# A residual stream kept token-major through both output projections, with the residual added by DMA

## The chip, the core and the metric

The kernel runs on one core of one Trainium2 chip. A core has a matrix engine (TensorE: PE in the profile, with PEld for the loading of its stationary operand), a vector engine (VectorE, DVE), a scalar engine (ScalarE, ACT), a general engine (GpSimd, POOL) and a sync engine (SyncE, SP) that here only issues DMAs. The metric is the device time of one execution in microseconds. Three runs of the kernel before took 2227.62, 2227.78 and 2229.94 us; their median is 2227.78 us.

## The reference

A trunk of two layers over 256 tokens of width D = 2048, in float32. `rms(x, w)` is x divided by the root of the mean of its squares, times the gains w.

```
h = x
h = h + (rms(gla(rms(h) @ w_in)) * silu(g)) @ gla_w_out     # gated linear attention, 4 heads
h = h + (silu(a) * u) @ w_down0     # a, u: the halves of a causal conv of width 3 over rms(h) @ w_up0
k, v = rms(h) @ kv_w                # shared keys and values, 16 heads of 128
q = rms(h) @ moba_w_q
h = h + softmax(q k' + bias) v @ moba_w_out                 # 256 tokens: own block only, causal
h = h + (silu(a) * u) @ w_down1
```

`gla_w_out` and `moba_w_out` are 2048 x 2048, each `w_up` is 2048 x 11264, each `w_down` 5632 x 2048.

## The kernel before

**Products.** Every weight is float32 and is used in two float32r parts: `whi`, the rounded weight, and `wlo`, what the rounding left. Activations are kept in the same two parts. A product takes three terms: hi x hi, lo x hi, hi x lo.

**The weight stream.** `WeightStream` (line 55) fetches weights from HBM in chunks of 128 x 2048 floats (1 MB) on SP's queue into three raw buffers. A chunk is split in halves of 1024 columns: ACT casts (line 126), DVE subtracts (line 127). Half n is what step n of the kernel multiplies; `step()` hands it out, and it runs the jobs that `after(n, job)` has put off by n steps. Halves are split two to three steps ahead. Chunk c + 4 is asked for when chunk c has been split.

**Two forms of product.** `gemm` (line 298) is feature-major: the weight is the stationary operand and the activations are streamed, hi and lo together as 512 columns against `whi` (line 305), then hi alone as 256 columns against `wlo` (line 307). A step is 8 + 8 matmuls, and four steps give 256 output features of all 256 tokens. `gemm_tok` (line 311) and `down` (line 625) are token-major: the activation is stationary and 512 weight columns are streamed, 12 matmuls a step.

`down` computes each down projection in two blocks of 1024 outputs. It takes the hidden features 256 at a time (index k, 22 of them). A plain k is 24 matmuls. A k marked with + in `ORDERS` uses a Strassen-like form of seven block products instead of eight: 21 matmuls, in four steps of 3, 6, 6 and 6. That form needs sums of the weight's quarters (`t13`, `t24`: `_sums`, lines 99 to 101, on DVE) and sums of the activation's quarters (`combine`, line 577, on DVE and ACT). The sums of accumulators that the form leaves are made after the last + (`u_sums`). The last k of a block, the tail, come in two passes (f = 0, 1), so that half of the outputs are complete before the other half.

**The residual.** It lives feature-major in `h` (eight pairs of 128 features, 256 tokens each). Both output projections, `go` and `mo`, use `gemm` in `project` (line 568), 8 x 4 steps each: `residual` adds the product into `h` with two DVE additions per pair, `make_xw` makes the next stage's operand from `h`, and `add_squares` sums squares over the pairs. The first down projection comes out token-major; `back` (line 762) turns it with 32 TensorE transposes, adds it into `h`, and `h` goes to DRAM (`hspill`) and comes back, since on-chip space is short meanwhile. In the second layer `turn_h` (line 715) turns `h` with 32 more transposes into DRAM (`hscr`), and `last_down` fetches it and adds it on DVE.

**The norms.** A `Norm` collects squares and makes the root as a row over tokens (`token_rstd`: a sum over partitions by a matmul with ones, then `rsqrt` with tables on ACT), as two columns (`column_rstd`), or both.

**Order of the work.** The order on an engine is not the program's alone: the file is planned by the language's scheduler, which issues what it holds ready first, earlier work preferred. SP carries the weight stream, POOL's queue the DMAs of `hspill`, `hscr` and the bias. PSUM gives three accumulators of two banks and two single banks. Large tiles come from one pool of 34 slots, small ones from a pool of six.

Of the kernel before, what the change touches and what calls it, by code (L numbers as in the profile page):

```python
# [37 lines left out]
def _order(text):  # L38

    return [(int(k.rstrip("+")), k.endswith("+")) for k in text.split()]  # L40
# [3 lines left out]
ORDERS = [[_order("0 2 4 1+ 6 3+ 8 5+ 10 7+ 12 16 9+ 14 11+ 17 13+ 18 15+ 19 20 21"),  # L44
           _order("0 2 4 6 8 1+ 10 3+ 12 5+ 14 7+ 16 9+ 17 11+ 18 13+ 19 15+ 20 21")],
          [_order("0 2 4 1+ 6 3+ 8 5+ 10 7+ 12 16 9+ 14 11+ 17 13+ 18 15+ 19 20 21"),
           _order("0 1+ 2 3+ 4 5+ 6 7+ 8 16 9+ 10 11+ 12 17 13+ 14 15+ 18 19 20 21")]]


def _tail(order):  # L50

    return min(3, len(order) - 1 - max(i for i, (_, seven) in enumerate(order) if seven))


class WeightStream:
# [19 lines left out]
    def add_quads(self, w, g, order):  # L75

        for i, (_, seven) in enumerate(order):
# [65 lines left out]
def trunk(ctx: ExitStack, tc: tile.TileContext, xT, cst, msk, w1p, w2a, w_k, w_qa, w_v2, w_v, w_g, w_go,  # L143
# [20 lines left out]
    def bank(name, shape):  # L164
        return mis_ps.tile(list(shape), F32, name=name, tag="bank")

    ws = WeightStream(tc, raw, parts)
    plan = [(w_v2, 1, 16384), (w_v, 2, 8192), (w_k, 4, 4096), (w_qa, 4, 4096), (w_g, 8, 4096), (w_go, 8, 4096),
            (w_up0, FT, 4096), (w_dn0, 2, None),
            (w_mq, 4, 8192), (w_kk, 4, 8192), (w_kv, 4, 8192), (w_mo, 8, 4096),  # L170
            (w_up1, FT, 4096), (w_dn1, 2, None)]
    for w, groups, cols in plan:
        for g in range(groups):
            if cols:
                ws.add(w, g, cols)
            else:
                ws.add_quads(w, g, ORDERS[int(w is w_dn1)][g])
# [7 lines left out]
    one = keep.tile([128, 1], F32, name="one")  # L185
# [3 lines left out]
    V.memset(one, 1.0)  # L189
# [4 lines left out]
    V.memset(mhalf, -0.5)  # L194
# [12 lines left out]
    def load_rest():  # L207
# [3 lines left out]
        nc.sync.dma_start(mk, msk)  # L211

    ws.lead[7, 0] = [load_rest]
# [7 lines left out]
    def make_xw(p, c, name):  # L221
        x = slot([128, 2, 2 * S], F32R, name)
        for i in range(2):
            n = col(c + 2 * p + i)
            hi = A.activation(x[:, i, :S], h[p][:, i, :], AF.Copy, scale=n)  # L225
            ws.first = ws.first or hi.ins
            V.scalar_tensor_tensor(x[:, i, S:], h[p][:, i, :], n, x[:, i, :S].bitcast(F32),
                                   op0=OP.mult, op1=OP.subtract)
        return x

    def add_squares(p, acc):
        if p == 0:
            with tc.issue_after(ws.first):
                A.activation(acc, h[p], AF.Square)
        else:
            sq = temp("hsq")
            A.activation(sq, h[p], AF.Square)
            V.tensor_add(acc, acc, sq)
# [19 lines left out]

    def token_rstd(acc, columns):
        ps = bank("sum_h", (128, S + 2))  # L260
        V.tensor_add(acc[:, 0], acc[:, 0], acc[:, 1])
        spread_sum(ps[:, :S], acc[:, 0])
        n = S + 2 if columns else S
        if columns:
            sum_columns(ps[:, S:], acc)
        r = small.tile([128, S + 2], F32, name="rstd_h")
        rsqrt(r[:, :n], ps[:, :n], 1.0 / D, (128, n))
        return r[:, :S], r[:, S:]

    def sum_columns(ps, acc):  # L270
        for t in range(2):
            T.matmul(ps[:, t:t + 1], acc[:, 0, 128 * t:128 * t + 128], one, start=True, stop=True)

    def column_rstd(acc):
        ps = bank("sum_h", (128, 2))
# [778 lines left out]
```

## Time and profile before

| | |
|---|---|
| median of three runs | 2227.78 us |
| profiled execution | 2229.07 us, of it 2227.3 us span |
| PE busy | 2217.3 us, 100% of the span |
| DVE, ACT, POOL busy | 1647.8, 1266.6, 44.1 us |
| DMA | 428.51 MB, mean 192 GB/s |
| granted TensorE clock | 1.0 |

The span reaches from the first to the last instruction of the profiled execution. The share of the busy time is an average over the stages. Matmuls overlap in the pipeline, so their listed durations are longer than the pace at which they follow each other; the pace is read from the starts of successive matmuls in the timeline. Groups name a line, an engine and tiles as out<-in.

### The profile page before, as it was taken

The page shows a single profiled execution, that of the slowest core. Times are in us where ns is not written, and L with a number is a line of the kernel's source. Part 1 is how long each engine was busy: PE and PEld are TensorE (multiplying, and loading weights), DVE is VectorE, ACT ScalarE, POOL GpSimd, SP SyncE. Part 2 cuts the span into 40 slices and gives each one's busy share as a digit, 9 for nine tenths or more (in the row PEclk, how much of TensorE's full clock was granted, in tenths as well). Part 3 has the DMA queues.
Part 4 walks back from the last instruction along what each step waited for, and adds up shares of the span by engine and source line. Part 5 has one row for each costly group of instructions (what it writes and reads, how often), then busy time and mean ns, then how long its engine had stood idle before and what let it go on. Part 6 is the DMA issues. An engine that isn't in the chain of part 4 may idle for free.

```text
span 2227.3 us, 30386 instructions
## 1 busy us (share of the span) xinstructions
PE 2217.3 (100%) x11776; PEld 1908.2 (86%) x11776; DVE 1647.8 (74%) x2279; ACT 1266.6 (57%) x1754; POOL 44.1 (2%) x60
## 2 busy tenths in 40 slices
PE   9999999999999999999999999999999999999999
PEld 7889888888888888888888888888888888888887
DVE  6666776777777777978866676567777777779886
ACT  6655654655555555555456665446555555555553
POOL 0000000000000000000010000000000000000000
PEclk9999999999999999999999999999999999999999
DMA  7553556555555555555555444556555555556654
GB/s 278 172 188 133 186 196 212 190 187 188 188 188 189 188 190 196 201 219 204 210 204 203 171 158 164 172 190 202 201 188 188 187 189 188 189 196 218 233 192 162
DMA packets 63300, 428.51 MB, mean 192 GB/s; under 512 B 7554, under 2 KB 8082, under 8 KB 13107
## 3 DMA queue, kind: packets, MB, share of 16 engines
q1 hardware_dynamic: 59346, 415.43, 53.8%
q0 software_dynamic: 3232, 10.56, 1.4%
q8 instruction: 92, 1.51, 0.3%
q10 hardware_dynamic: 576, 0.58, 0.1%
q14 instruction: 54, 0.43, 0.1%
HBM read 420.23 MB, written 6.32 MB: 192 GB/s over the span
## 4 chain that ended last, share of the span: by engine, by line
PE 96%; DMA 2%; DVE 1%; issue 1%; ACT 0%; DVEq 0%; ACTq 0%
PE acc L305 40%; PE acc L307 21%; PE acc L655 11%; PE acc L320 11%; PE p L655 7%; PE acc L323 5%; DMA wraw<-w_dn 2%; DVE wlo L127 1%; PE sT L510 0%; PE tr L848 0%; PE s L866 0%; PE pT L886 0%; DVE t L100 0%; PE z L416 0%; PE s L864 0%
## 5 line engine op out<-in xcount | busy, mean ns | idle before, releaser
L127 DVE TENSOR_TENSOR wlo<-wraw,whi 128x1024 fp32r<-128x1024 f32 (+1 forms) x785 | 935.7, 1199 | 423.9 <-ACT whi L126 405.0
L126 ACT CAST whi<-wraw 128x1024 fp32r<-128x1024 f32 (+1 forms) x785 | 805.2, 1032 | 740.8 <-PE acc L305 457.0
L305 PE MATMUL acc<-xw,whi 128*128 128x512 f32 x3328 | 854.4, 393 | 0.0
L305 PEld LDWEIGHTS acc<-xw,whi 128*128 128x128 f32 x3328 | 590.8, 189 | 98.8
L307 PEld LDWEIGHTS acc<-xw,wlo 128*128 128x128 f32 x3328 | 468.4, 190 | 41.7
L307 PE MATMUL acc<-xw,wlo 128*128 128x256 f32 x3328 | 481.6, 282 | 0.0
L655 PE MATMUL acc<-whi,hid 128*128 128x512 f32 x576 | 183.0, 390 | 0.0
L655 PE MATMUL p<-whi,hid 128*128 128x512 f32 x512 | 166.4, 389 | 0.0
L320 PE MATMUL acc<-whi,xw 128*128 128x512 f32 x512 | 130.2, 395 | 5.1 <-ACT xw L225 5.1
L320 PE MATMUL acc<-whi,xkv 128*128 128x512 f32 x512 | 133.6, 394 | 0.0
L655 PEld LDWEIGHTS acc<-whi,hid 128*128 128x128 f32 x576 | 107.8, 188 | 22.2
L320 PEld LDWEIGHTS acc<-whi,xw 128*128 128x128 f32 x512 | 96.4, 190 | 25.1 <-ACT xw L225 5.1
L655 PEld LDWEIGHTS p<-whi,hid 128*128 128x128 f32 x512 | 96.1, 188 | 20.1
L126 ACT CAST whi<-t 128x1024 fp32r<-128x1024 f32 x64 | 66.4, 1052 | 80.1 <-PE p L655 50.3
L320 PEld LDWEIGHTS acc<-whi,xkv 128*128 128x128 f32 x512 | 94.3, 188 | 18.4
L609 ACT ACTIVATE au<-up,cs 128x256 f32<-128x256 f32 x176 | 96.4, 595 | 21.7 <-DVE up L605 21.7
L655 PE MATMUL acc<-wlo,hid 128*128 128x512 f32 x288 | 95.7, 390 | 0.6 <-DVE wlo L127 0.5
L127 DVE TENSOR_TENSOR wlo<-t,whi 128x1024 fp32r<-128x1024 f32 x64 | 77.7, 1220 | 16.2 <-ACT whi L126 9.4
L655 PE MATMUL p<-wlo,hid 128*128 128x512 f32 x256 | 84.6, 390 | 0.0
L655 PE MATMUL acc<-whi,comb 128*128 128x512 f32 x256 | 83.4, 389 | 0.0
L613 DVE SCALAR_TENSOR_TENSOR au<-up,cs,au 128x254 f32<-128x254 f32 x176 | 77.3, 477 | 0.0
L611 DVE SCALAR_TENSOR_TENSOR au<-up,cs,au 128x255 f32<-128x255 f32 x176 | 76.8, 477 | 0.0
(256 smaller groups left out, 1997.6 us busy)
## 6 DMA issues: line engine op xcount, KB each, us to landing
wraw<-w_up SPq DMA_DIRECT2D x176, 1024.0 KB, 4.8
wraw<-w_dn SPq DMA_DIRECT2D x88, 1024.0 KB, 4.9
wraw<-w_g SPq DMA_DIRECT2D x16, 1024.0 KB, 4.8
wraw<-w_go SPq DMA_DIRECT2D x16, 1024.0 KB, 4.8
wraw<-w_mq SPq DMA_DIRECT2D x16, 1024.0 KB, 4.9
wraw<-w_kk SPq DMA_DIRECT2D x16, 1024.0 KB, 4.9
wraw<-w_kv SPq DMA_DIRECT2D x16, 1024.0 KB, 4.8
wraw<-w_mo SPq DMA_DIRECT2D x16, 1024.0 KB, 4.8
```

The lines of the kernel that those rows point to most:

```text
L126: nc.scalar.copy(hi[:, a:b], src[:, a:b])
L127: nc.vector.tensor_sub(lo[:, a:b], src[:, a:b], hi[:, a:b].bitcast(F32))
L305: T.matmul(ps[:, b, :], hi[:, c:c + 128], xs(kt), start=kt == 0, stop=False)
L307: T.matmul(ps[:, b, :S], lo[:, c:c + 128], xs(kt)[:, :S], start=False, stop=kt == kts - 1)
L320: T.matmul(ps[:, t, :], xs(kt)[:, x0 + 128 * t:x0 + 128 * t + 128], hi[:, c:c + 512], start=kt == 0 and x0 == 0, stop=False)
L323: T.matmul(ps[:, t, :], xs(kt)[:, 128 * t:128 * t + 128], lo[:, c:c + 512], start=False, stop=kt == KT - 1)
L609: A.activation(au[:, i, :], t[:, i, :], AF.Identity, bias=col(cb + n), scale=col(cw + 2 * 2 * FT + n))
L611: V.scalar_tensor_tensor(au[:, i, 1:], t[:, i, :S - 1], col(cw + 2 * FT + n), au[:, i, 1:], op0=OP.mult, op1=OP.add)
L613: V.scalar_tensor_tensor(au[:, i, 2:], t[:, i, :S - 2], col(cw + n), au[:, i, 2:], op0=OP.mult, op1=OP.add)
L655: T.matmul(p[n], x[xi], w[wi][:, 512 * f:512 * f + 512], start=n not in begun, stop=left[n] == 0)
```

## The change

`go` and `mo` take the form of the down projections, and `h` is no longer kept. All four stages that end in a residual sum work alike:

- `down` serves `go` and `mo` too, with their own orders of eight k, two of them marked + in each block. The orders of the two down projections are rewritten, with an explicit bar ahead of the tail.
- After the last + of a block, four token-major sums `r` are made, and four DMAs on POOL's queue add the old residual to them (`accum_op=OP.add`): for `go` from the input `x_tok`, then from the rows that the stage before wrote. At the end of a tail pass DVE adds the accumulator to `r`, which completes the residual.
- `onward` then writes the complete rows to DRAM on POOL's queue, squares them on ACT with a running sum along the row, and turns them by TensorE transposes; the next operand is made from PSUM. `TURNS` says in which block and at which position the turns stand.
- A norm is a column from these sums (`close`, power of -0.5 on POOL). Where a row over tokens is needed, `spread` makes it from a diagonal tile and a matmul with ones.
- The first norm takes its squares from `x_tok`, 2 MB that SP's queue loads in four DMAs behind chunk 7 (program order). `turn_h`, `project`, `residual`, `add_squares`, `token_rstd` and `column_rstd` go. `hspill` is written from the turned tiles in the first down projection and fetched for the keys' operand; the bias is made 11 steps earlier; two pairs of attention outputs borrow an accumulator.

```diff
+ORDERS = {
+    "go": [_order("0 1+ 2 3+ 4 | 5 6 7"), _order("0 2 1+ 3+ 4 | 5 6 7")],
+    "dn0": [_order("0 2 4 1+ 6 3+ 8 5+ 10 7+ 12 9+ 14 11+ 16 13+ 17 15+ 18 | 19 20 21"),
+            _order("0 2 4 6 1+ 8 3+ 10 5+ 12 7+ 14 9+ 16 11+ 17 13+ 18 15+ 19 | 20 21")],
+    "mo": [_order("0 2 1+ 3+ 4 | 5 6 7"), _order("0 2 1+ 3+ 4 | 5 6 7")],
+    "dn1": [_order("0 2 4 1+ 6 3+ 8 5+ 10 7+ 12 9+ 14 11+ 16 13+ 17 15+ 18 | 19 20 21"),
+            _order("0 1+ 2 3+ 4 5+ 6 7+ 8 9+ 10 11+ 12 13+ 14 15+ 16 17 18 | 19 20 21")],
+}
+TURNS = ((0, (1, 2)), (0, (1, 2)), (1, 1), (1, 1), (1, (1, 2)), (1, (1, 2)))
...
         nc.sync.dma_start(mk, msk)
+        for c in range(4):
+            xt.append(slot([128, 2, 512], F32, "xt"))
+            nc.sync.dma_start(xt[c], x_tok[:, :, 512 * c:512 * c + 512].rearrange("t p f -> p t f"))
...
+        def square(self, t, c, src):
+            A.activation(temp("junk", (128, 512)), src, AF.Square, accum_out=self.ss[:, t, c:c + 1])
         def close(self):
+            m = small.tile([128, 2], F32, name="m_n")
+            self.col = small.tile([128, 2], F32, name="col_n")
+            V.tensor_reduce(m, self.ss, axis=AX.X, op=OP.add)
+            V.tensor_scalar(m, m, 1.0 / D, EPS, op0=OP.mult, op1=OP.add)
+            nc.gpsimd.tensor_tensor(self.col, m, mhalf[:, :2], op=OP.pow)
+        def spread(self):
+            d = temp("diag", (128, 2, 128))
+            for t in range(2):
+                V.tensor_scalar(d[:, t], ident, self.col[:, t:t + 1], None, op0=OP.mult)
+            ps = bank("row", (128, S))
+            spread_sum(ps, d.rearrange("p a b -> p (a b)"))
+            self.rstd = small.tile([128, S], F32, name="rstd_h")
+            A.copy(self.rstd, ps)
...
-    def project(xs, kts, norms):
-        for p in range(NP):
-            ps = gemm(xs, kts)
-            residual(ps, p)
-            for n in norms:
-                n.feed(p)
...
                 if i == last:
-                    sums = ready(b, p)
+                    r = [temp(f"c{n}", (128, 512)) for n in range(4)]
+                    A.copy(r[0], p[1])
+                    V.tensor_add(r[1], r[0], p[6])
+                    V.tensor_add(r[2], r[1], p[7])
+                    V.tensor_add(r[1], r[1], p[5])
+                    V.tensor_add(r[3], r[2], p[5])
+                    for n in (0, 2, 1, 3):
+                        nc.gpsimd.dma_start(r[n], res(n // 2, 2 * b + n % 2), accum_op=OP.add)
...
                 for t, n in enumerate(ns):
+                    V.tensor_add(r[2 * t + f], r[2 * t + f], p[n])
+                    done(t, 2 * b + f, r[2 * t + f])
...
+        def done(t, c, x):
+            sums[t, c] = x
+            nc.gpsimd.dma_start(keep_row(t, c), x)
+            nrm.square(t, c, x)
         def back(q, where):
             tp = where()
             for i in range(2):
                 for t in range(2):
+                    f = 128 * (q % 2 * 2 + i)
+                    T.transpose(tp[:, i, 128 * t:128 * t + 128], sums[t, q // 2][:, f:f + 128], ident)
+            nrm.operand(q, tp)
...
+        for q in range(len(at), NP):
+            after(1 if feature_major else q - 3, lambda q=q: back(q, in_bank))
+        after(2 if feature_major else 3, nrm.close)
+        if feature_major:
+            after(3, nrm.spread)
...
-    project(rows(go), KT, [n_ffn])
+    middle("go", go, go_sums, from_input, n_ffn, rows1, TURNS, True)
...
-    project(rows(ox), KT, [n_ffn])
-    for c in range(4):
-        for t in range(2):
-            after(6 + 2 * (2 * c + t), lambda c=c, t=t: turn_h(c, t))
+    middle("mo", ox, {}, rows2, n_ffn, rows3, TURNS, True)
```

More of the change, by code (lines that the diff above doesn't have):

```diff
@@ L372, in trunk @@
     for p in range(2, NP):
-        after(2 * p - 3, lambda p=p: nrm.operand(p))
-    for p in range(NP):
-        after(8 + p, lambda p=p: add_squares(p, nrm.acc))
-    after(17, nrm.close)
+        after(2 * p - 3, lambda p=p: nrm.operand(p, h[p]))
+    for c in range(4):
+        for t in range(2):
+            after(8 + 2 * c + t, lambda c=c, t=t: nrm.square(t, c, xt[c][:, t]))
+    after(16, nrm.close)
+    after(17, nrm.spread)
     xs = rows(nrm.xs)
@@ new lines, in trunk, with from_input, last_down, done @@
+    rows1, rows2, rows3 = scratch("rows1"), scratch("rows2"), scratch("rows3")
+    hspill = dram.tile([NP, 128, 2 * S], F32, name="hspill")
+    def from_input(t, c):
+        return x_tok[t, :, 512 * c:512 * c + 512]
+    def last_down(hid, sums):
+        def done(t, c, x):
+            (A if t and c % 2 else nc.sync).dma_start(out[t, :, 512 * c:512 * c + 512], x)
+        down("dn1", hid, sums, rows3, done, {})
+    n_ffn = Norm(C_FN, "xw")
+    middle("go", go, go_sums, from_input, n_ffn, rows1, TURNS, True)
```

302 lines of the change are left out of this document (104 added, 198 removed).

## The prediction

> **What bounds the kernel now.** First the page's busy times, then the waits of TensorE and of its weight loads.
>
> ```profile
> PE 2217.3 (100%) x11776; PEld 1908.2 (86%) x11776; DVE 1647.8 (74%) x2279; ACT 1266.6 (57%) x1754; POOL 44.1 (2%) x60
> ```
>
> ```profile
> PE acc L320 <- ACT xw L225: 5.1, 1, 5.1
> PE acc L655 <- DVE wlo L127: 0.5, 1, 0.5
> ```
>
> ```profile
> PEld acc L655 <- DVE wlo L127: 2.7, 6, 0.9
> ```
>
> TensorE is never without work: it waits 5.1 us once, for the first operand, and 0.5 us later. Whatever else the change does, the time follows the sum of matmul work plus new waits of TensorE. So I need the pace of both forms, which the starts in the timeline give: first a `gemm` step at the border of `go` and the up projection, then a step of `down` near the end.
>
> ```profile
> 387.71 2.00 PE L305 MATMUL acc<-xw,whi 128*128 128x512 f32 x8
> 389.56 1.12 PE L307 MATMUL acc<-xw,wlo 128*128 128x256 f32 x8
> 390.51 2.00 PE L305 MATMUL acc<-xw,whi 128*128 128x512 f32 x8
> ...
> 2218.95 1.07 PE L655 MATMUL acc<-whi,hid 128*128 128x512 f32 x4
> 2219.86 0.62 PE L655 MATMUL acc<-wlo,hid 128*128 128x512 f32 x2
> 2220.31 1.07 PE L655 MATMUL acc<-whi,hid 128*128 128x512 f32 x4
> 2221.22 0.62 PE L655 MATMUL acc<-wlo,hid 128*128 128x512 f32 x2
> 2221.67 1.07 PE L655 MATMUL acc<-whi,hid 128*128 128x512 f32 x4
> ```
>
> ```profile
> L305 PE MATMUL acc<-go,whi x256: 387/393/398, 298.3 to 387.0; 128*128 128x512 f32 x128
> ```
>
> A `gemm` step takes 390.51 - 387.71 = 2.80 us for 6144 streamed columns; `go` fills 387.7 - 298.3 = 89.4 us with 32 of them. A plain step of `down`, also 6144 columns but in 12 matmuls, takes 2221.67 - 2218.95 = 2.72 us: 0.2267 us a matmul.
>
> **The change part by part.** *1. The two projections.* Each has per block two k of 21 matmuls and six of 24, that is 186, and 372 in two blocks: 372 x 0.2267 = 84.3 us against 89.4 (32 steps of 2.795). That is 5.1 to 5.2 us less for each projection, 10.4 for both taken with the unrounded pace: 2.7 each from the 12 matmuls left out, 2.5 each from the better pace. All of it is on the path.
>
> By the Trainium skill ("TensorE: Matmul & The Clock Gate", section "Wait — 56ns, not 53.3ns?") warm matmuls follow each other at their columns over 2.4 GHz plus about 2.5 ns; that would make 215.8 and 109.2 ns of the two sizes, 2.60 us of a `gemm` step, 2.59 of a `down` step, and only 2.9 us gained a projection, 5.9 for both. The trace disagrees (2.80 and 2.72).
>
> *2. Transposes.* `go`, the first down projection and `mo` turn 32 tiles each, where before the first down projection and `turn_h` did: 32 more, eight groups of four.
>
> ```profile
> 1121.26 2.09 PE L320 MATMUL acc<-whi,xw 128*128 128x512 f32 x8
> ...
> 1124.09 0.60 PE L769 MATMUL hf<-mk,c 128*128 128x128 f32 x4
> 1124.45 2.10 PE L320 MATMUL acc<-whi,xw 128*128 128x512 f32 x8
> ...
> 1127.30 1.98 PE L320 MATMUL acc<-whi,xw 128*128 128x512 f32 x8
> 1130.02 1.98 PE L320 MATMUL acc<-whi,xw 128*128 128x512 f32 x8
> ...
> 1134.78 0.50 PE L272 MATMUL sum_h<-one,acc_sq 128*128 128x1 f32 x4
> 1135.14 0.96 PE L323 MATMUL acc<-wlo,xw 128*128 128x512 f32 x3
> ```
>
> A step with one group takes 1124.45 - 1121.26 = 3.19 us, one without 1130.02 - 1127.30 = 2.72: 0.47 a group, 8 x 0.47 = +3.8 us.
>
> *3. Norms.* The matmuls for columns go (1135.14 - 1134.78 = 0.36 us, for two norms): -0.7 us. The three rows over tokens still cost two matmuls each. The new chain (squares, reduce, power on POOL, diagonal, split, sum) has three to four steps' time, since the first up tile of four steps is scaled only after 11.2 us: nothing. If a matmul of `spread` stood too early in TensorE's queue it would hold up all behind it for the rest of that chain, a microsecond or two; POOL's two row writes stand ahead of the power. The removed additions only relieve DVE.
>
> *4. Sevens in the projections.* These shift load to DVE.
>
> ```profile
> L127 DVE TENSOR_TENSOR wlo<-wraw,whi 128x1024 fp32r<-128x1024 f32 x751 | 914.8, 1222 | 422.3 <-ACT whi L126 403.8 <-PE acc L323 5.3 <-PE acc L307 3.8
> L99 DVE TENSOR_TENSOR t<-wraw 128x1024 f32<-128x1024 f32 x32 | 39.1, 1222 | 27.6 <-DMA wraw<-w_dn 27.6
> L100 DVE TENSOR_TENSOR t<-t,wraw 128x512 f32<-128x512 f32 x32 | 21.9, 684 | 0.1
> ```
>
> ```profile
> 298.20:387.70 89.50, 89.50 (x514) 78.66 (x514) 60.02 (x72) 44.74 (x57) 3.83 (x7) 1.00 0.61 209
> 880.20:995.00 114.80, 114.80 (x509) 95.07 (x508) 101.50 (x125) 63.91 (x71) 0.56 (x2) 1.00 0.57 202
> 1993.60:2108.00 114.40, 114.40 (x507) 94.63 (x507) 103.60 (x130) 62.74 (x70) 4.30 (x8) 1.00 0.63 221
> ```
>
> The windows give busy time of PE, PEld, DVE, ACT, POOL. A seven costs DVE four splits (three of 1.222 and one of half the width, 0.684 like line 100) and three sums (1.222 + 2 x 0.684): 6.9 us, while TensorE needs 21 x 0.2267 = 4.8; a plain k costs 2.4 against 5.4. A projection thus asks 4 x 6.9 + 12 x 2.4 = 56 us of DVE for weights. Eight sums of accumulators and six of the eight final additions (0.68 each) make it 66, twelve low parts of operands (estimated at 0.5, since twice the width takes 0.684) 72: of 88 us, 82%. The blocks of the down projections ran at 88% (101.50 of 114.80) and 91% without a listed wait of TensorE worth the name. Bounds: 0, and 2.2 us for each of eight sevens, 17 us, if nothing were split ahead. The nearest row is the 2.7 us that weight loads waited for DVE over 32 sevens (line 99 counts them): 0.08 each, 8 x 0.08 = +0.7 us. The rewritten orders of the down projections spend a spare plain k earlier or later; with two residual additions fewer on DVE around the sums I take nothing for them, between -2.7 (all of that wait goes) and +2.7 (it doubles).
>
> *5. Residual by DMA.* Per block POOL issues four accumulating loads and, in three stages, four writes of rows; `hspill` keeps its 16 issues, `hscr` loses its 16: 72 against 32 on an engine that is 2% busy. No trace row shows an accumulating load; plain ones bound it from below.
>
> ```profile
> h<-hspill POOLq DMA_DIRECT2D x8, 256.0 KB, 6.2
> bias<-bscr POOLq DMA_DIRECT2D x4, 512.0 KB, 7.6
> ...
> res<-hscr POOLq DMA_DIRECT2D x8, 256.0 KB, 4.4
> ```
>
> The same 256 KB land in 4.4 or 6.2 us; doubled, since the destination is read as well, 12.4. In `go` one plain k and three tail steps lie between the last seven and the first addition that needs the result: 5.4 + 8.2 = 13.6 us; in block 1 of the first down projection 10.9. The copy and the four sums that feed it take some 5 x 0.68 = 3.4 us. So 6.2 lands in time, 12.4 makes DVE wait 2 to 5 us, and behind that addition stand splits of weights, of which TensorE has three plain steps, 8.2 us, in hand. Cost on the path: nothing, up to a wait of that length.
>
> *6. The start.* `x_tok` adds 2.1 MB to SP's queue while the DMA engines are full.
>
> ```profile
> 20.00:25.00 5.00, 5.00 (x24) 4.14 (x23) 5.00 (x9) 3.97 (x6) 0.00 (x0) 1.00 1.03 407
> ```
>
> ```profile
> 16.57 0.33 SPq L209 DMA_DIRECT2D w2s<-w2a  x1
> 20.27 57.67 SPq L89 DMA_DIRECT2D wraw<-w_v  x11
> ```
>
> ```profile
> 29.84 2.00 ACT L126 CAST whi<-wraw 128x1024 fp32r<-128x1024 f32 x2
> ```
>
> ```profile
> 32.24 3.79 PE L320 MATMUL acc<-whi,xw 128*128 128x512 f32 x16
> ```
>
> At 410 GB/s it takes 5.1 us. `w2s`, which the program loads with chunk 7, was issued at 16.57, ahead of chunk 5 (20.27). If `x_tok` goes the same way, chunk 5 lands 5.1 us later. Its first half is cast by 31.84 and used by the second eight matmuls of the last row, at 32.24 + 8 x 0.227 = 34.05: slack 2.2, so TensorE waits 2.9 us. If it is issued after chunk 6, none. Bounds 0 and 5.1; I take the middle of the two cases, +1.5.
>
> *7. Borders.* From the end of `go` the operand of the last two pairs needs two additions, eight transposes, four casts and four subtractions before step 3 (8.4 us): hidden, at worst about a microsecond a border. The border before the queries loses two DVE instructions a pair. Bias, `hspill` and borrowed accumulators move among covered work: nothing.
>
> Sum: -10.4 + 3.8 - 0.7 + 0.7 + 1.5 = -5.1 us. The profiled execution took 2229.1 us (1.8 around its span of 2227.3), 1.3 above the median of the runs shown; against itself 2224.0, against the median **2222.7 us**. The bound of what can be told from no change is 0.2%, 4.5 us: below 2223.3 is faster, above 2232.2 slower.
>
> **The rivals.** *A, within 0.2%: the gain is spent on new waits.* Consecutive sevens (`1+ 3+`), `x_tok` ahead of chunk 5 and a late `spread` each take a few microseconds. For it: 6.9 against 4.8 us at a seven, and a start whose slack is 2.2 us. Against it: the 88 to 91% blocks, which alternate in the same way. From 0.6 us more than in the sum it decides; typically sevens 2.9, start 2.9, two rows over tokens 1 each: -7.3 + 7.8, 2228.3 us.
>
> *B, slower: accumulating loads land late.* Then DVE stands at the addition, splits stop, and after 8.2 us in hand TensorE stops too, in seven blocks (the last one's tail is longer). With 4 us for the sums, the path is touched from a landing of 13.6 - 4 + 8.2 = 17.8 us, and decides from -5.1 + 7 x (L - 17.8) = 4.5, L = 19.2. At 21 us: 2222.7 + 22 = 2245 us. For it: nothing shows such a load, and weights come beside it at 200 GB/s. Against it: three to four times the plain 4.4 and 6.2 are needed. The Trainium skill ("SBUF — State Buffer", section "SBUF: two separate sides") speaks for it: POOL's DMAs have their descriptors written by POOL itself, which a DVE instruction in a two-port mode locks out. The plain loads above landed in 4.4 to 6.2 us beside a DVE at 88 to 91%, so the trace does not bear it out for this mix of instructions.
>
> *C, within 0.2%: the pace per column does not change in the projections.* 372 x 512 columns at 2.795/6144 us are 86.6 us, 2.8 less a projection instead of 5.2, and the sum -0.3: 2227.5 us. Against it: 2.72 is the pace of the second form in this trace. By the pitch of the Trainium skill, above, the sum would be -5.9 + 3.8 - 0.7 + 0.7 + 1.5 = -0.6, 2227.2 us.
>
> **How the numbers follow.** The forecast has 0.53, A 0.27, B 0.08, C 0.02; 0.10 is for several waits that together exceed 0.2% without B. Faster 0.54 with a little of the small cases, same 0.30, slower 0.16. The forecast's own range is 2218 (no new wait, and the old 2.7 us gone) to 2223.3. The range to 8 in 10 takes in A and the lower part of the slower cases: 2218 to 2233.
>
> **What would show it.** In the profile after, `go` from its first to its last matmul should take about 88 us with its turns and `mo` about 90; waits of TensorE on DVE should stay under 2 us a projection; accumulating loads should land within 13 us of issue; the first stage should show at most 3 us of waiting for a weight cast. It is wrong if TensorE waits for `c` sums or `wlo` in every block, if the token-major steps run slower than 2.75 us, or if the start loses more than 3 us.

## The result and the profile after

The changed kernel took 2234.69 us (median of ten runs, 2233.36 to 2237.60) where the kernel before, on the same chip, took 2229.40 (2227.58 to 2230.29): a ratio of 1.0028 with the 95% interval 1.0020 to 1.0037. It is slower, by a little more than the 0.2% that can be told from no change. The forecast was 2222.7 us, the range 2218 to 2233. The profiled execution of after took 2233.36 us with a span of 2231.6; before it was 2229.07 and 2227.3. So 4.3 us came where 5.1 should have gone, and 9.4 us have to be explained.

The busy times of the page after, and the waits of TensorE (us in total, times, longest):

```profile
PE 2213.3 (99%) x11520; PEld 1891.8 (85%) x11520; DVE 1656.6 (74%) x2293; ACT 1277.0 (57%) x1799; POOL 81.5 (4%) x103
```

```profile
PE acc L297 <- ACT xw L235: 6.5, 2, 5.2
PE acc L630 <- ACT whi L129: 3.6, 4, 1.5
PE acc L630 <- DVE wlo L130: 2.0, 3, 0.9
PE acc L630 <- DVE ox L319: 1.0, 1, 1.0
PE acc L297 <- ACT whi L129: 0.5, 1, 0.5
PE acc L692 <- DVE c L671: 0.2, 1, 0.2
```

The busy time of TensorE is smaller than before (2217.3), and yet the span is longer. Before, the list had 5.1 us for the first operand and 0.5 us beside it; now 6.6 us of waits stand at the matmuls of `down` (line 630), 1.3 us at another operand and 0.5 us in the first stage. Windows over the stages of after (length, then busy time of PE, PEld, DVE, ACT, POOL, clock, DMA share, GB/s) say where. They are `go`, the first up projection, the queries, `mo` and the second up projection:

```profile
298.91:389.51 90.60, 87.94 (x394) 71.58 (x393) 67.94 (x80) 49.23 (x66) 10.99 (x15) 1.00 0.69 227
389.51:883.23 493.72, 493.72 (x2831) 433.99 (x2830) 372.68 (x555) 286.89 (x409) 1.25 (x2) 1.00 0.56 189
...
1111.03:1206.96 95.93, 94.61 (x436) 77.59 (x434) 60.99 (x75) 56.73 (x89) 20.79 (x26) 1.00 0.71 241
1408.93:1504.07 95.14, 90.97 (x413) 73.68 (x412) 67.69 (x80) 50.02 (x69) 10.45 (x14) 1.00 0.66 214
1504.07:1997.79 493.72, 493.72 (x2831) 433.99 (x2830) 374.31 (x556) 289.08 (x412) 1.79 (x3) 1.00 0.55 189
```

TensorE stands still in `go`, in the queries and in `mo`; in both up projections, borders and rows over tokens included, it never does. The busy time still covers a part of each wait, since a matmul's listed duration is longer than the pace. Below, waits are therefore counted from start to start of successive matmuls, less the pace, where the excess is over 0.15 us: 3.3 us in `go`, 5.2 in `mo`, 1.5 in the queries, 1.0 in the first stage and 0.7 in the last, 11.7 in all, against 1.4 before (both in the down projections; the slow first 5 us of TensorE's work are left out on both sides). The waits grew by 10.3 us. What is left of the difference, 4.3 - 10.3, is -6.0 us: TensorE's work did become shorter.

A profile is one execution, and the executions of one kernel range over 1 to 7 us in the tables below. In the eight edited kernels of the first two tables, PE, ACT and DVE run the first 37 us in the same order as here, yet the wait near 35 us took 0.3 to 1.7 us. In the last down projection the changed kernel and those with the bias later, with the turns moved and with both edits run one order too, and their waits there were 0.7, 2.3, 0.6 and 2.0 us. So a difference of one or two microseconds between two profiles, in a stage that was not edited, shows no cause.

The stretch in `go` in which its waits lie, in the timeline of after: first TensorE, then ACT, then DVE (start, duration, engine, line, operation; idle time before it and what ended that in brackets).

```profile
350.19 0.61 PE L630 MATMUL p<-wlo,go 128*128 128x512 f32 x2
352.03 0.73 PE L630 MATMUL acc<-whi,go 128*128 128x512 f32 x2 [1.22 <-ACT whi L129]
...
356.98 0.60 PE L692 MATMUL acc<-mk,c 128*128 128x128 f32 x4
358.05 0.50 PE L630 MATMUL acc<-whi,comb 128*128 128x512 f32 x1 [0.47 <-ACT whi L129]
...
361.89 0.50 PE L630 MATMUL acc<-wlo,comb 128*128 128x512 f32 x1 [0.87 <-DVE wlo L130]
```

```profile
348.12 0.48 ACT L235 ACTIVATE xw<-acc,cs 128x256 fp32r<-128x256 f32 x1 [0.66 <-PE acc L692]
349.98 1.05 ACT L129 CAST whi<-t 128x1024 fp32r<-128x1024 f32 x1 [1.39 <-PE p L630]
350.94 1.04 ACT L129 CAST whi<-wraw 128x1024 fp32r<-128x1024 f32 x1
```

```profile
357.35 1.22 DVE L102 TENSOR_TENSOR t<-wraw 128x1024 f32<-128x1024 f32 x1
358.48 1.22 DVE L130 TENSOR_TENSOR wlo<-wraw,whi 128x1024 fp32r<-128x1024 f32 x1
359.62 0.48 DVE L237 SCALAR_TENSOR_TENSOR xw<-acc,cs,xw 128x256 fp32r<-128x256 f32 x1
360.01 0.68 DVE L103 TENSOR_TENSOR t<-t,wraw 128x512 f32<-128x512 f32 x1
360.61 1.22 DVE L130 TENSOR_TENSOR wlo<-t,whi 128x1024 fp32r<-128x1024 f32 x1
```

At 350 us the cast that TensorE needs next (`whi<-wraw`) stands on ACT behind the cast of a sum for a later half (`whi<-t`), which itself waited 1.39 us for a buffer that TensorE had to free. From 357 on DVE is busy without a gap, with the sums of the second of two neighbouring sevens (`1+ 3+`); the low part of a turn's operand (line 237) stands between a sum and its next step, and TensorE waits for the parts one by one. `mo` repeats this: at 1464.54 the cast of a sum (there it waited 1.64 us for DVE's sum) again stands ahead of the one that TensorE needs, and from 1471.93 on the sums of the second seven do. At this point it is not yet shown which of the things that meet here has to go: the neighbouring sevens, the turns, or the loads that run beside them.

One wait in `mo`, 1.2 us in its first seven, is of another kind:

```profile
1425.05 1.22 DVE L102 TENSOR_TENSOR t<-wraw 128x1024 f32<-128x1024 f32 x1
1426.18 0.68 DVE L319 TENSOR_TENSOR ox<-acc,ox 128x512 fp32r<-128x512 f32 x1
1426.92 1.20 PE L630 MATMUL acc<-whi,comb 128*128 128x512 f32 x4 [1.00 <-DVE ox L319]
```

These matmuls do not read `ox`. They are the first to write the third accumulator, which the last two pairs of attention outputs had borrowed, and DVE reads it out (line 319) only behind a sum of the seven (line 102).

The accumulating loads, which no row of before showed (KB each, median us from issue to landing):

```profile
c<-rows POOLq DMA_DIRECT2D x24, 256.0 KB, 9.7
c<-x_tok POOLq DMA_DIRECT2D x8, 256.0 KB, 8.5
```

### The profile page after: what moved, and what is told of

The parts are those of the page before. It is cut to its first block, busy times and chain, and to the rows that moved or that the text cites. A ratio compares the mean times of both kernels' runs of the same rounds, so it can differ in the third digit from the quotient of the medians.

```text
span 2231.6 us, 30038 instructions
## 1 busy us (share of the span) xinstructions
PE 2213.3 (99%) x11520; PEld 1891.8 (85%) x11520; DVE 1656.6 (74%) x2293; ACT 1277.0 (57%) x1799; POOL 81.5 (4%) x103
## 4 chain that ended last, share of the span: by engine, by line
PE 94%; DMA 3%; DVE 2%; issue 1%; ACT 1%; SPq 0%; POOL 0%; DVEq 0%; ACTq 0%; POOLq 0%
PE acc L282 34%; PE acc L284 18%; PE acc L630 15%; PE acc L297 10%; PE p L630 9%; PE acc L300 5%; DMA wraw<-w_dn 1%; DVE wlo L130 1%; DMA c<-rows 1%; DMA w2s<-w2a 0%; DMA cs<-cst 0%; ACT whi L129 0%; PE sT L495 0%; PE tr L784 0%; PE s L802 0%
## 5 line engine op out<-in xcount | busy, mean ns | idle before, releaser
L129 ACT CAST whi<-t 128x1024 fp32r<-128x1024 f32 x80 | 84.1, 1053 | 87.6 <-PE p L630 53.8
L630 PEld LDWEIGHTS p<-whi,hid 128*128 128x128 f32 x512 | 96.1, 188 | 20.1
L130 DVE TENSOR_TENSOR wlo<-t,whi 128x1024 fp32r<-128x1024 f32 x80 | 97.4, 1223 | 15.4 <-ACT whi L129 10.2
L630 PE MATMUL acc<-whi,comb 128*128 128x512 f32 x320 | 104.7, 392 | 2.2 <-DVE ox L319 1.0
```

The source lines that it names most:

```text
L129: nc.scalar.copy(hi[:, a:b], src[:, a:b])
L130: nc.vector.tensor_sub(lo[:, a:b], src[:, a:b], hi[:, a:b].bitcast(F32))
L630: T.matmul(p[n], x[xi], w[wi][:, 512 * f:512 * f + 512], start=n not in begun, stop=left[n] == 0)
```

## The experiments

All changes are against the changed kernel unless another is named. The first four try the loads, the order, the bias and the form of the addition; the next four take apart the turns and the sevens; the last four join what was found. The tables hold the median with its range, the ratio to the kernel before with its interval, and the length of `go`, `mo` and the queries' stage with the waits in it (before: 89.5, 91.8 and 94.9 us, no waits).

**Plain loads**

```diff
-nc.gpsimd.dma_start(r[n], res(n // 2, 2 * b + n % 2), accum_op=OP.add)
+nc.gpsimd.dma_start(r[n], res(n // 2, 2 * b + n % 2))
```

> Here the four residual loads of a block are plain loads of the same bytes into the same tiles: they overwrite the sums of the products where the changed kernel adds to them, so the stages that follow compute on the residual and the last products alone; every instruction stands where it stood. Theory L (accumulating loads are slow): loads land in 4 to 6 us instead of 8.5 to 9.7, the additions at the end of a tail pass no longer make VectorE wait 2 to 6 us, and TensorE's waits in the two projections, 3.6 us in go and 5.1 in mo, fall to under 1 and under 2; the time falls by 4 to 7 us against the changed kernel, to about 2229. Theory S (the two neighbouring sevens alone ask more of VectorE than the time gives): the loads land sooner, but TensorE still waits about 3 us after the border of the blocks in each projection, and the time falls by less than 1.5 us.

**Sevens apart, by a plain k from the tail**

```diff
-    "go": [_order("0 1+ 2 3+ 4 | 5 6 7"), _order("0 2 1+ 3+ 4 | 5 6 7")],
+    "go": [_order("0 1+ 2 3+ 4 | 5 6 7"), _order("0 2 1+ 4 3+ 5 | 6 7")],
...
-    "mo": [_order("0 2 1+ 3+ 4 | 5 6 7"), _order("0 2 1+ 3+ 4 | 5 6 7")],
+    "mo": [_order("0 2 1+ 3+ 4 | 5 6 7"), _order("0 2 1+ 4 3+ 5 | 6 7")],
...
-TURNS = ((0, (1, 2)), (0, (1, 2)), (1, 1), (1, 1), (1, (1, 2)), (1, (1, 2)))
+TURNS = ((0, (1, 2)), (0, (1, 2)), (1, 1), (1, 1), (1, (1, 1)), (1, (1, 1)))
```

> The second blocks of both projections keep their work but not their order: 0 2 1+ 4 3+ 5 ahead of a tail of 6 7, so that a plain k of 5.4 us stands between the two sevens. Theory S: TensorE's waits after the border (some 3.6 us in go, 3.6 in mo) go to under 1 us each and the time falls by 5 to 6 us. Theory L: VectorE still stands 5 us at the additions of block 0, and its lag is only caught up later: half of the waits remain, the time falls by 2 to 3 us.

**The bias later**

```diff
-    after(1, bias_rows)
+    after(12, bias_rows)
```

> The bias of the attention is made 12 steps into the queries again, as before the change, not 1 step. If its small matmul and its bank of PSUM stand in the way of the last two turns (the 1.3 us that TensorE waits for an operand of the queries in the changed kernel), that wait goes and the time falls by 1.3 to 1.6 us. If the late turns come from the late residual instead, the wait stays and the time is the changed kernel's within 0.5 us.

**The residual added on DVE**

```diff
-                    A.copy(r[0], p[1])
-                    V.tensor_add(r[1], r[0], p[6])
...
+                        nc.gpsimd.dma_start(r[n], res(n // 2, 2 * b + n % 2))
+                    u2, u3 = temp("u2", (128, 512)), temp("u3", (128, 512))
+                    A.copy(u2, p[1])
+                    V.tensor_add(r[0], r[0], p[1])
+                    V.tensor_add(u2, u2, p[6])
+                    V.tensor_add(u3, u2, p[7])
+                    V.tensor_add(r[2], r[2], u3)
+                    V.tensor_add(u2, u2, p[5])
+                    V.tensor_add(u3, u3, p[5])
+                    V.tensor_add(r[1], r[1], u2)
+                    V.tensor_add(r[3], r[3], u3)
```

> The residual is fetched by plain loads into the tiles of r, and VectorE adds the products to it: eight additions and one copy a block instead of four and one, 2.7 us more of VectorE in each of eight blocks. Theory L: nothing waits for a load any more, VectorE's 2.7 us a block are fewer than the 5 it stood, and the time falls by 2 to 5 us. Theory S: VectorE is what is short in the projections, so the waits grow by up to 2.7 us a projection and the time rises by 2 to 5 us.

| edit | us (range) | ratio (interval) | `go` (waits) | `mo` (waits) | queries (waits) |
|---|---|---|---|---|---|
| the changed kernel | 2234.69 (2233.36–2237.60) | 1.0028 (1.0020–1.0037) | 90.6 (3.3) | 95.1 (5.2) | 95.9 (1.5) |
| plain loads | 2232.09 (2231.48–2233.13) | 1.0015 (1.0006–1.0023) | 90.6 (3.3) | 94.4 (4.5) | 95.9 (1.5) |
| sevens apart, tail of two | 2237.31 (2235.89–2242.60) | 1.0045 (1.0032–1.0059) | 87.9 (1.4) | 92.0 (2.8) | 95.9 (1.5) |
| bias later | 2233.38 (2231.35–2235.07) | 1.0022 (1.0013–1.0031) | 90.8 (3.5) | 94.4 (4.5) | 95.8 (1.2) |
| added on DVE | 2234.90 (2233.77–2235.51) | 1.0028 (1.0017–1.0038) | 90.6 (3.3) | 94.4 (4.5) | 95.9 (1.5) |

With plain loads, which leave out the sums that they overwrite, the landing falls by 3.0 and 3.6 us:

```profile
c<-rows POOLq DMA_DIRECT2D x24, 256.0 KB, 6.7
c<-x_tok POOLq DMA_DIRECT2D x8, 256.0 KB, 4.9
```

but in `go` the waits stay where they were, to a few hundredths of a microsecond, and in `mo` they fall by 0.7 us of 5.2. The kernel with the bias later shows the same 4.5 us in `mo`, with accumulating loads and the same order there, so even the 0.7 are not shown to be the loads' doing. The late residual is not what stops TensorE in the two projections; what else stands in the engines' order has to be it. The whole fell by 2.6 us, between the two theories (less than 1.5, and 4 to 7): the accumulation does cost something, and the profiles do not say where. The addition on DVE speaks the same way on the waits: four more additions a block, and the same 3.3 us in `go`. Its time stayed, where one theory had 2 to 5 us less and the other 2 to 5 us more.

With the sevens apart the waits in the second of the two neighbouring sevens go in both projections (1.9 us each), and the one at 350 stays. But the tail has one k less, and the operand of the up projection is late: that stage takes 499.7 us instead of 493.7, the second one 497.7. Windows of this kernel at the border show what happens:

```profile
390.00:395.00 5.00, 3.62 (x23) 2.79 (x21) 2.93 (x6) 2.51 (x6) 1.77 (x3) 1.00 0.33 128
395.00:400.00 5.00, 2.93 (x7) 2.00 (x8) 3.86 (x7) 1.86 (x4) 0.03 (x1) 0.73 0.59 200
```

TensorE is idle for 1.4 and 2.1 us, and in the second window its granted clock drops to 0.73. What was gained in the projections is lost at the border, with interest: the whole rose by 2.6 us, where both theories had it fall.

The bias made later removes the wait of 1.5 us in the queries' stage, for which its place ahead of the last turns is to blame, but one of 1.2 us appears at the stage's start; that one returns below. That the time fell by 1.3 us, as expected, is in part luck: `mo` lost 0.7 us of waits and the last stage gained 1.6.

The next four edits set theory N, that the neighbouring sevens are the cause, against rival T, that the turns are.

**Sevens apart, with the tail kept**

```diff
-    "go": [_order("0 1+ 2 3+ 4 | 5 6 7"), _order("0 2 1+ 3+ 4 | 5 6 7")],
+    "go": [_order("0 1+ 2 3+ 4 | 5 6 7"), _order("0 1+ 2 3+ 4 | 5 6 7")],
...
-    "mo": [_order("0 2 1+ 3+ 4 | 5 6 7"), _order("0 2 1+ 3+ 4 | 5 6 7")],
+    "mo": [_order("0 2 1+ 3+ 4 | 5 6 7"), _order("0 1+ 2 3+ 4 | 5 6 7")],
```

> Both blocks of mo and the second of go take the order that the first block of go has: 0 1+ 2 3+ 4, then the tail of three, so no two sevens are neighbours and the tail keeps its length. Theory N (neighbouring sevens: DVE needs 6.9 us for each, TensorE 4.8): the waits of 1.94 us in go and of 1.95 us in mo that lie in the second of two neighbouring sevens go, nothing comes back at the border, the whole is about 4 us below the changed kernel, near 2231. Rival T (the turns at position 1 put two casts and two low parts ahead of the sums of a seven): since position 1 is now itself a seven, the waits move to it and stay within 1 us of their old sum, 3.3 in go and 4.5 in mo.

(In `mo` the edit reaches the second block alone; its first block keeps its order, other than the text above says.)

**The turns moved**

```diff
-TURNS = ((0, (1, 2)), (0, (1, 2)), (1, 1), (1, 1), (1, (1, 2)), (1, (1, 2)))
+TURNS = ((0, (1, 2)), (0, (1, 2)), (1, (0, 1)), (1, (0, 2)), (1, (1, 2)), (1, (1, 2)))
```

> The orders of the changed kernel; the third and fourth group of turns leave position 1 of the second block and go to its first tail pass. Theory T: the waits in the second block go (3.3 us in go, 3.6 in mo), the whole about 6 us below the changed kernel, near 2229. Theory N: the waits of the neighbouring sevens stay (1.94 us in go, 1.95 in mo), at most the one ahead of them (1.38 and 1.64) goes: at most 3 us gained.

**Both**: the two diffs together.

> Both edits together: no neighbouring sevens, and the third and fourth group of turns in the first tail pass. If the waits of TensorE in the two projections have these two causes and no third, go and mo show under 1 us of waiting and the whole is 7 to 8 us below the changed kernel, near 2227, within 0.2% of the kernel before. If DVE's whole load in the projections is what counts (72 of 88 us), the waits only move, and less than half of that is gained.

**One seven less**

```diff
-    "go": [_order("0 1+ 2 3+ 4 | 5 6 7"), _order("0 2 1+ 3+ 4 | 5 6 7")],
+    "go": [_order("0 1+ 2 3+ 4 | 5 6 7"), _order("0 2 1+ 3 4 | 5 6 7")],
...
-    "mo": [_order("0 2 1+ 3+ 4 | 5 6 7"), _order("0 2 1+ 3+ 4 | 5 6 7")],
+    "mo": [_order("0 2 1+ 3+ 4 | 5 6 7"), _order("0 2 1+ 3 4 | 5 6 7")],
```

> The second block of go and of mo has one seven instead of two (0 2 1+ 3 4, then the tail): three more matmuls each, 0.7 us a projection. Theory N: the 1.94 us in go and the 1.95 us in mo go, the 1.38 and 1.64 us ahead of the first seven stay: 2.5 us below the changed kernel. Theory T: the waits behind the turns stay in the first seven, 3 us each: no gain, 1.4 us lost.

| edit | us (range) | ratio (interval) | `go` (waits) | `mo` (waits) | queries (waits) |
|---|---|---|---|---|---|
| sevens apart | 2234.42 (2232.67–2236.56) | 1.0026 (1.0016–1.0036) | 89.8 (2.5) | 95.0 (4.8) | 97.3 (2.7) |
| turns moved | 2229.46 (2227.75–2231.02) | 1.0003 (0.9994–1.0011) | 89.1 (1.9) | 92.5 (2.5) | 96.0 (1.5) |
| both | 2229.85 (2228.26–2231.18) | 1.0006 (0.9997–1.0015) | 87.2 (0.2) | 92.7 (2.9) | 97.9 (3.3) |
| one seven less | 2229.93 (2229.19–2232.00) | 1.0008 (0.9999–1.0016) | 89.0 (1.4) | 92.4 (1.9) | 96.1 (1.5) |

Taking the sevens apart alone gains nothing: theory N by itself falls. The waits move to the seven that now stands where the turns are, as rival T said. Moving the turns alone takes the kernel back to the time of before, about 5 us, as T forecast (though only 4.1 of the 6.9 us of waits went that it counted on), and in the waits of TensorE with that edit `wlo` is nearly gone:

```profile
PE acc L297 <- ACT xw L235: 6.2, 2, 4.8
PE acc L630 <- ACT whi L129: 2.9, 2, 1.7
PE acc L297 <- ACT whi L129: 1.5, 1, 1.5
PE acc L630 <- DVE ox L319: 1.0, 1, 1.0
PE acc L630 <- DVE wlo L130: 0.2, 1, 0.2
```

But T alone isn't the whole either: it forecast that the waits of the second blocks go, and one of 1.9 us in `go` and of 1.4 in `mo` is left, the cast behind another half's cast. In `go` that last one goes when both edits are made; in `mo` 1.0 us is left at the parts of a seven and 0.7 us comes up at an addition. And one seven less, with the turns left where they are, does as much as the move: 4.8 us, where T had no gain and N 2.5. Two neighbouring sevens without the turns pass but for that cast, and so does one seven behind the turns; the turns with two sevens, neighbours or not, do not: it takes both. In `mo` the 1.2 us at the borrowed accumulator stayed through all of these but the last (0.5).

Both edits together do not beat the turns alone in the whole; the two ranges overlap. In the profile the 2.0 us that `go` gains beyond the turns alone are given back: 1.8 us at the end of the first down projection, and the last stage shows 2.0 us of waits against 0.6. In both places the engines run the same instructions in the same order as in the changed kernel, so the order there is not the cause. The timeline of the kernel with both edits at the first of them, TensorE and DVE:

```profile
1109.03 0.61 PE L300 MATMUL acc<-wlo,xw 128*128 128x512 f32 x2
1111.29 1.20 PE L630 MATMUL acc<-whi,hid 128*128 128x512 f32 x4 [1.64 <-DVE c L671]
```

```profile
1103.41 1.22 DVE L130 TENSOR_TENSOR wlo<-wraw,whi 128x1024 fp32r<-128x1024 f32 x1
1110.55 0.69 DVE L671 TENSOR_TENSOR c<-c,acc 128x512 f32<-128x512 f32 x1 [5.92 <-issue]
```

DVE has nothing to do for 5.9 us; it stands at the first addition of the tail, whose accumulating load was issued at 1100.74 and landed at 1110.47, and TensorE waits behind it. The load took 9.7 us here as in the changed kernel, but it was issued 6.5 us ahead of the stage's end where there it was 9.3: the casts ahead of it had waited longer for a weight chunk. ACT in the changed kernel, then with both edits:

```profile
1096.27 2.95 ACT L129 CAST whi<-wraw 128x1024 fp32r<-128x1024 f32 x3 [2.31 <-DMA wraw<-w_dn]
```

```profile
1095.26 2.95 ACT L129 CAST whi<-wraw 128x1024 fp32r<-128x1024 f32 x3 [5.10 <-DMA wraw<-w_dn]
```

This goes for all nine accumulating kernels: in the four in which that load landed at most 1.3 us behind the stage's end TensorE did not wait, and in the five in which it landed 2.7 to 3.6 us behind it waited 1.2 to 2.2. Why the chunk came later in some of them was not tested.

**The version with all edits**, in two steps. First both edits of `go` (`mo` keeps its orders, and its turns move), and `x_tok` behind weight chunk 6 on SP's queue:

```diff
-                self.nc.sync.dma_start(t[:, a:b], rows[:, a:b])
+                self.sent = self.nc.sync.dma_start(t[:, a:b], rows[:, a:b])
+                self.by = getattr(self, "by", {})
+                self.by[self.n_dma] = self.sent
...
-            nc.sync.dma_start(xt[c], x_tok[:, :, 512 * c:512 * c + 512].rearrange("t p f -> p t f"))
+            with tc.issue_after(ws.by[6].ins):
+                nc.sync.dma_start(xt[c], x_tok[:, :, 512 * c:512 * c + 512].rearrange("t p f -> p t f"))
```

> Joins what the last runs gave: the third and fourth group of turns in the first tail pass, go with no neighbouring sevens in its second block, mo in its old orders, and the four loads of x_tok behind weight chunk 6 instead of ahead of chunk 5. Theory T with theory N behind it: go waits under 0.5 us as with both edits, mo 2.5 as with the turns alone. If x_tok ahead of chunk 5 delays the start, the wait near 35 us (0.7 to 1.5 us so far) goes; if the squares on ACT do it, it stays or moves to where the squares now stand. About 2226.5 us in all, 3 us below the run with the turns alone; without the effect at the start 2227.5.

Then the bias 12 steps into its stage, as above:

> The run before with the bias made 12 steps into the stage of the queries instead of 1. If the bias only stands in DVE's way, the wait of 1.5 us in that stage goes: 2225 us. If the wait at the end of the first down projection, which three of the earlier runs showed (1.1 to 1.8 us, for an accumulating load that landed 9 to 10 us after its issue), comes in its place, as with the bias alone: 2226.5 us.

And the same with plain loads:

> The run before with plain loads in place of the accumulating ones, instruction for instruction: the accumulators that the four sums hold are overwritten, so that part of the product is left out of the output. A wait at the end of the first down projection that is due to accumulating goes (plain loads landed in 4.9 to 6.7 us), worth 1.1 to 1.8 us if it is there; all other waits of TensorE stay as they are.

Last, with plain loads and the additions on DVE as above, and

```diff
-    tmp = ctx.enter_context(tc.tile_pool(name="tmp", bufs=6))
+    tmp = ctx.enter_context(tc.tile_pool(name="tmp", bufs=8))
```

> The whole computation again: the order of the work of the version with all three edits, with the residual loaded plainly into r and added on DVE with the sums (eight additions a block instead of four and a copy), and eight small tiles instead of six, since two more are alive. If the landing of the accumulating loads is what that version still loses against its twin with plain loads (3.5 us), this one comes out at 2224 to 2225 us, 0.2% below the kernel before, with no wait at the end of the first down projection. If DVE's room in the blocks is what counts, its three to four further additions (0.7 us each) in seven blocks bring new waits for weight parts: 2227 us or more.

| edit | us (range) | ratio (interval) | `go` (waits) | `mo` (waits) | queries (waits) |
|---|---|---|---|---|---|
| turns, `go`'s order, `x_tok` later | 2228.79 (2226.72–2229.57) | 0.9999 (0.9990–1.0007) | 88.2 (1.1) | 92.2 (2.5) | 98.0 (3.4) |
| and bias later | 2227.66 (2226.36–2230.53) | 0.9994 (0.9985–1.0003) | 87.5 (0.4) | 92.3 (2.6) | 96.8 (2.2) |
| and plain loads | 2224.14 (2223.79–2224.77) | 0.9979 (0.9970–0.9988) | 86.9 (0) | 91.9 (2.2) | 94.5 (0) |
| and added on DVE | 2223.38 (2222.80–2224.30) | 0.9975 (0.9965–0.9985) | 86.9 (0) | 91.9 (2.2) | 94.5 (0) |

With `x_tok` behind chunk 6 the wait near 35 us (0.3 to 1.7 us in the runs before) is gone in the first two of these kernels, and 0.2 and 0.5 us stand near 33 us in the last two. The squares on ACT move with the loads, so the times alone don't tell which of them made it. The traces say more: in the changed kernel the chunk that TensorE waits for, chunk 5, landed at 34.24 us (30.42 before the change, 29.91 in the first of these kernels), and ACT cast it at 34.79, right behind a square that had begun at 34.17. So the wait comes of the late chunk, and of the half microsecond that the square adds. The first step stays 2.3 us above what was expected; the border's wait is 1.9 of it. With the bias later its own wait goes, and that at the border is 2.2 us. In this version accumulating against plain loads is worth 3.5 us, more than the 1.1 to 1.8 expected, in two kernels that differ in nothing else and whose ranges do not meet: by the stages of one profile each 2.3 in the queries' (the border), 0.6 in `go`, 0.4 in `mo` and 0.8 in the last, less some tenths elsewhere. Since the plain twin leaves out part of the sum, the last run makes it whole. It is faster than the kernel before by 0.25%. That it comes out 0.7 us from the forecast confirms nothing: the forecast was for accumulating loads and for these turns where they stood. The two more small buffers were not tried alone. Its waits (its lines are three further down than in the changed kernel), the landing of its loads, and its windows of `go` and `mo`:

```profile
PE acc L300 <- ACT xw L238: 4.9, 1, 4.9
PE acc L633 <- DVE ox L322: 1.0, 1, 1.0
PE acc L633 <- ACT whi L131: 0.9, 1, 0.9
PE acc L300 <- ACT whi L131: 0.5, 2, 0.3
```

```profile
c<-rows POOLq DMA_DIRECT2D x24, 256.0 KB, 5.3
c<-x_tok POOLq DMA_DIRECT2D x8, 256.0 KB, 5.9
```

```profile
298.26:385.11 86.85, 86.85 (x395) 71.77 (x394) 73.12 (x89) 48.89 (x67) 5.37 (x10) 1.00 0.63 218
...
1402.99:1494.88 91.89, 90.00 (x414) 73.79 (x413) 74.22 (x90) 51.09 (x71) 5.38 (x10) 1.00 0.59 206
```

DVE is busier in both stages than in the changed kernel (73.1 and 74.2 us against 67.9 and 67.7) and TensorE waits less. So it is not the amount of DVE's work over the stage that made TensorE wait there.

## Why the prediction was wrong, point by point

It forecast -7.3 us of work and 2.2 us of new waits. The work came out at -6.0 and the waits at 10.3. Of the 8.1 us too much of waits, 6.6 lie with the sevens (point 4) and 2.7 with what point 7 called covered; the start (point 6) and the down projections took 0.5 and 0.7 less than forecast. The 1.3 us of work seem to be waits shorter than the 0.15 us from which they were counted: in the last version, which has the same matmuls, the same count gives -7.6.

**1 to 3, projections, transposes, norms: right.** `go` should be 84.3 us and 6 groups of turns 2.8, together 87.1; with no wait it took 86.85 in the last version. The pace held, so rival C falls. The second up projection, without `turn_h`, is 2.3 us shorter (496.0 to 493.7). No matmul of `spread` held up anything: both up projections are busy for their whole length.

**4, sevens in the projections: this is the step that failed.** The step is the price of a seven: it took 0.08 us each, 0.7 in all, from a row over the down projections, and looked at DVE's load averaged over the stage: 72 of 88 us forecast, 67.9 of 90.6 measured. The average was no worse than thought. What it left out is that four casts and four low parts of the turns are put into the stretch ahead of and inside two neighbouring sevens, and that ACT and DVE take their work in a fixed order. The term was 7.3 us, 3.3 in `go` and 4.0 in `mo`; the bound from above of 17 held it. Moving two groups of turns takes 4.1 of the 7.3, and one seven less in each second block 4.6, so neither is the cause without the other. What is left in `mo` with both edits (1.7 us beside the borrowed accumulator) no run explains. The forecast sign "waits of TensorE on DVE under 2 us a projection" would have missed half of it, since what is listed is as often a cast of ACT.

**5, residual by DMA: right on the waits of this profile, too kind as a rule.** The loads land in 8.5 and 9.7 us, far from rival B's 19.2, and in this execution their slack sufficed: taking the accumulation out leaves the waits in `go`. Yet the whole was 2.6 us shorter without it, so "nothing" was too little. (Of the plain loads that the prediction set beside a DVE at 88 to 91%, those of `hspill`, 994 to 1061 us, ran beside one at 80 to 82%.) In the second block of the first down projection, where the prediction put 10.9 us of cover, little was left, as DVE and TensorE show in the timeline of after:

```profile
1111.50 0.69 DVE L671 TENSOR_TENSOR c<-c,acc 128x512 f32<-128x512 f32 x1 [4.31 <-DMA c<-rows]
```

```profile
1113.29 1.07 PE L630 MATMUL acc<-whi,hid 128*128 128x512 f32 x4
```

The addition waited 4.3 us for its load, as the prediction had it (2 to 5), and ended 1.1 us before TensorE went on with that product. In the five kernels in which the load landed latest, 1.2 to 2.2 us of waiting showed at this place. The Trainium skill ("DMA: Bandwidth & Descriptors", section "Anatomy of one DMA — SWDGE (gpsimd) path") gives about 2.0 us and the bytes over 436 GB/s for a DMA issued by GpSimd, which makes an estimate of 2.6 us for 256 KB; here, beside the weight stream, even plain loads took 4.1 to 6.7 (medians of a run).

**6, the start: right in its mechanism, smaller in size.** `x_tok` was issued ahead of chunk 5, the worse of the two cases, and the chunk landed 3.8 us later than before (5.1 expected). The first stage had 1.0 us of waits, 0.7 of them at this chunk, where 2.9 was feared and 1.5 taken; about half a microsecond of the 0.7 is the square that stands on ACT ahead of the cast, which the prediction did not have.

**7, borders and the rest: mis-sized.** The borders of `go` and `mo` were covered, with a tail of three k: with two, TensorE lost 6 and 4 us. "Bias: nothing" was 1.5 us; making it later removes them, and which of its parts (its matmul, its bank, its copy on ACT) holds up the last turns was not separated. "Borrowed accumulators: nothing" was 1.2 us in `mo`, read from the trace above; no run gave those two pairs a place of their own.

**The rivals.** A is what happened in kind, waits that eat the gain (it had 7.8 us of new waits and 2228.3), but of its three parts only the sevens came, at 7.3 us for 2.9; the start took less and the rows over tokens nothing. The case of several waits together, given 0.10, is the one that came.

## What to carry to other kernels

When work is moved next to a stretch that already asks an engine for more than the matrix engine gives it time for (here 6.9 against 4.8 us), price it in that stretch and not in the stage's average: list what stands on each in-order engine between two steps of TensorE. A wait that is removed uncovers the next one, so a cover of "nothing" should be given with the microseconds that are left of it. Where the bytes are the same, a plain load and an addition on an engine with room can be cheaper than an accumulating load: 2223.38 against 2227.66 us in the last version, with two more small buffers, though 2234.90 against 2234.69, no gain, in the changed kernel itself.

## What the runs showed of the hardware beside that

An accumulating load of 256 KB took 6.8 to 10.0 us (medians of a run) where plain ones in the same places took 4.1 to 6.7. It also held POOL longer: 0.94 and 1.02 us an issue (medians, from `rows` and from `x_tok`) in the changed kernel against 0.54 in its plain twin.

The clock of TensorE fell after short pauses. In the kernel with the tail of two, two listed waits within five microseconds were followed by matmuls at a granted clock of 0.50, as its timeline and its windows show:

```profile
392.45 1.09 PE L692 MATMUL hf<-mk,c 128*128 128x128 f32 x8 [1.34 <-DVE c L671]
...
396.87 0.84 PE L282 MATMUL acc<-xw,whi 128*128 128x512 f32 x2 [1.91 <-DVE xw L237]
```

```profile
398.00:399.00 1.00, 1.00 (x3) 0.81 (x4) 1.00 (x1) 0.23 (x1) 0.00 (x0) 0.50 1.04 434
399.00:400.00 1.00, 1.00 (x4) 0.81 (x3) 0.51 (x2) 0.00 (x0) 0.00 (x0) 0.50 1.00 426
```

The Trainium skill ("TensorE: Matmul & The Clock Gate", section "HAM oscillation — how this bites in real kernels") puts the limit at idle gaps of about 3.4 us; no single gap here was that long, and here the measurement decides.

The length of a gap does not decide it alone. At the border of `mo` in the same kernel listed gaps of 1.25 and 0.31 us, a microsecond apart, were followed by two microseconds at 0.50. In the version with the bias later and accumulating loads a listed gap of 2.0 us, at the end of the first down projection, was followed by a clock of 1.00. What does decide it no run here shows.
